# A recorder with its own list schedule takes the place of the framework's scheduler, on one core

## The chip, the cores and the metric

The kernel runs on one core of a Trainium2 chip. The core has TensorE (matmuls, in the profile PE, with its weight loads as PEld), VectorE (DVE), ScalarE (ACT), GpSimd (POOL) and SyncE (SP), which issues all DMA transfers here. Each engine takes its own instructions in a fixed order and waits on semaphores where an instruction needs another engine's or a transfer's result. The metric is the device time of one execution in microseconds; less is better.

## The reference

Two blocks over 2048 tokens of width 1024, all in float32. The first is an RMS norm, a pooling mixer and a residual; the second has modulation by a condition vector, a mixer of two halves and a residual.

```python
def pool_mixer(h, in_w, group_w, group_b, scale, out_w):
    u, gate = jnp.split(h @ in_w, 2, axis=-1)
    ug = u.reshape(b, s, POOL_GROUPS, POOL_GROUP_DIM)
    pooled = jnp.stack([trailing_mean(ug[:, :, g], w) ...], axis=2) - ug
    mixed = jnp.einsum('bsgc,gcd->bsgd', pooled, group_w) + group_b
    return (mixed.reshape(b, s, POOL_WIDTH) * scale * jax.nn.silu(gate)) @ out_w

def hybrid_mixer(h, w_in, b_in, conv_w, conv_b, rpb, ml_norm_w, w_out):
    proj = h @ w_in + b_in
    (na_q, na_k, na_v, na_z, ml_q, ml_k, ml_v, ml_o, ml_z, i_f, f_f, i_b, f_b) = jnp.split(proj, ...)
    na_out = neighbourhood_attention(na_q, na_k, na_v, rpb) * jax.nn.silu(na_z)
    qk = jax.nn.silu(centred_short_conv(jnp.concatenate([ml_q, ml_k], axis=-1), conv_w, conv_b))
    h_fwd = mlstm_chunkwise(mq, mk, mv, i_f, f_f)
    h_bwd = flip(mlstm_chunkwise(flip(mq), flip(mk), flip(mv), flip(i_b), flip(f_b)))
    hm = (h_fwd + h_bwd) * jax.nn.sigmoid(ml_o)      # then a layer norm per head, times silu(ml_z)
    return jnp.concatenate([na_out, ml_out], axis=-1) @ w_out
```

The attention has 8 heads of 64 on a grid of 32 rows by 64 columns; each token sees a window of 8 by 16, with a bias table. The mLSTM has 4 heads of 128, in both directions, chunk by chunk, with a state that each chunk hands to the next.

## The kernel before

Projections keep float32 accuracy with three matmuls each: weights and activations are split into a high and a low part (`split`, L140 on ScalarE and L141 on VectorE), and high x high, high x low and low x high are summed in PSUM. `load_w` (L153) brings a weight piece to `wraw` (2 buffers) by DMA and splits it into `whl` (4 buffers); `proj_cm` (L176 to L178), `proj_ko` (L165 to L167) and `tm_chunk` (L645 to L647, 256 columns) are the matmuls. Results go to the core's DRAM space and are read back by the stages that follow.

The program has these stages in time. Up to some 600 us the first block, in two halves of 1024 tokens. Then the second block's projections (`cm_chunk`, `tm_chunk`), the output half-stages (`out_half`, `out_block`) and the last norm. From some 830 us to 1890 us the projections are laced with two other kinds of work:

- 16 calls of `na_pair`, with 128 attention blocks between them. A block is: two matmuls of scores L735 into one PSUM bank; L738 on VectorE adds the bias tile `bt` and takes the row maximum; L741 on ScalarE is the exponential, L742 and L743 (POOL) the division; L749 on TensorE transposes; L752 (ScalarE), L753 (VectorE) and L754 (POOL) copy and split the result; L761 on TensorE multiplies with the values; L765 to L767 combine. Scores and transposes have one PSUM bank each, so the next block's L735 waits for L738, and its L749 for L752.
- 32 calls of `ml_step`. Each loads `ui` (L886, a row of 512 numbers for every partition, 256 KB), takes an exponential of it with `dec` as bias on ScalarE (L890), multiplies on POOL (L891, L892), takes another exponential (L894) and has small matmuls L916, L917, L924. `ml_gates` runs twice before such steps; it stores `d_u` and `d_dc` (L854 to L856), which `ui` and `dec` (L857) read back.

The order of each engine is set by the framework's scheduler. The program gives every operation a priority: a running number that `prio(base)` sets to another base for a block of code. The framework has its own model of the machine's times, takes the operations that are ready in it by priority, and writes each engine's instructions in that order. Attention and mLSTM bases (1900000 to 2550000) are mostly lower numbers, thus earlier, than those of the projections laced with them (2100000, 3000000, 3600000). In the output stage `out_norm` (L1026, the chain L186 to L191, and eight multiplications L1033 on POOL) is laced with `out_block` (L1056, the matmuls L1059 to L1061, L1063, and the sums L1069 on POOL).

Of the kernel before, what the change touches and what calls it, by code (L numbers as in the profile page):

```python
# [1 line left out]

# [4 lines left out]
F32 = mybir.dt.float32  # L7
F32R = mybir.dt.float32r
I32 = mybir.dt.int32
AF = mybir.ActivationFunctionType  # L10
ALU = mybir.AluOpType
PSUM = bass.MemoryType.PSUM
DRAM = bass.MemoryType.DRAM
# [48 lines left out]
KCW = (24, 32, 32, 24)  # L62
CC = (0, 1, 1, 2)
CCW = (24, 32, 24)


def body(nc, tc, a, out):
# [64 lines left out]

    d_b = [[dp.tile([8, 8, 16, (12, 16, 12)[e] * CCW[x]], F32, name=f"d_b{e}_{x}") for x in range(3)] for e in range(3)]
    mod = cp.tile([128, 24], F32, name="mod")
# [147 lines left out]
    def tables(x, tb, cs2):  # L282
        W = CCW[x]
        m0 = (0, 24, 56)[x]
        tv = tb[:, 0:23 * W].rearrange("p (a b) -> p a b", b=W)
        sh = (0, -8, -8)[x]

        def put(e, r, c0, a0, n):
            nc.sync.dma_start(d_b[e][x][:, r, :, c0 * W:(c0 + n) * W], tb[:, a0 * W:(a0 + n) * W])  # L289

        for h in range(8):
            nc.sync.dma_start(tv[h * 16:h * 16 + 16, 4:19],
                              bass.AP(tensor=a["rpb"].tensor, offset=16 + sh + 465 * h, ap=[[1, 16], [31, 15], [1, W]]))
        mk = cs2[:, C_CM + m0:C_CM + m0 + W]
        nc.gpsimd.tensor_tensor(out=tv[:, 4:19], in0=tv[:, 4:19],
                                in1=mk[:, None, :].to_broadcast([128, 15, W]), op=ALU.add)
        for r in range(4):
            put(0, 4 + r, 0, 8 + r, 8)
            put(2, r, 4, 4 + r, 8)
        for r0, r1 in ((0, 7), (15, 23)):  # L300
            nc.gpsimd.memset(tv[:, r0:r1], NEG)
        for r in range(8):
            put(1, r, 0, r, 16)
        for r in range(4):
            put(0, r, 0, 4 + r, 12)
            put(0, 4 + r, 8, 16, 4)
            put(2, 4 + r, 0, 4 + r, 12)
            put(2, r, 0, 0, 4)
# [963 lines left out]
```

## Time and profile before

| | before |
|---|---|
| median of 3 runs | 2161.88 us (2161.3 to 2164.38) |
| profiled execution | 2162.99 us, span 2161.2 us |
| TensorE busy | 1938.7 us (90%) |
| VectorE, ScalarE, POOL busy | 1266.6, 858.1, 676.7 us |
| DMA, all engines | 60.2% of the span, 406.18 MB |
| granted TensorE clock, mean | 0.946 |

The span is the time between the first and the last instruction. A matmul's busy time as the profile models it overlaps with the next one's, so the pace of TensorE is read from how many matmuls a stretch with no idle time holds. The granted clock has two levels, 1.2 and 2.4 GHz; 1.00 is the higher one, and a mean of 0.94 says how long each was granted. In lists of waits a row names who stood idle, what ended it, and the total, the count and the longest.

### The profile page before, as it was taken

To read this page: it belongs to the slowest core of one execution; us is meant where nothing else is said; L and a number is where in the kernel's file an instruction comes from. 1 tells how busy PE (TensorE), PEld (TensorE's weight loads), DVE (VectorE), ACT (ScalarE), POOL (GpSimd) and SP (SyncE) were. 2 spreads that over 40 slices of the span, in tenths; PEclk is the share of its full clock that TensorE was granted. 3 is DMA by queue.
4 is the path that set the end of the run, shared out by engine and by line. 5 is a ranking of instruction groups with operands and counts; after the bars stand their busy time and mean duration, and the time that the engine had idled before them with its cause. 6 is when DMAs were issued, how large, how long until landed. Compare 5 with 4: busy or idle time off the path is not lost.

```text
span 2161.2 us, 29857 instructions
## 1 busy us (share of the span) xinstructions
PE 1938.7 (90%) x10246; PEld 1659.6 (77%) x10246; DVE 1266.6 (59%) x2688; ACT 858.1 (40%) x1779; POOL 676.7 (31%) x624
## 2 busy tenths in 40 slices
PE   8999889999899799799999799878868788998997
PEld 6877768788789688789898687777867666877875
DVE  6654574786825474355556478544546668747565
ACT  3221233333422234444443344455444456544442
POOL 1110064353540002313233343344443345410252
PEclk8999999999999899999999899989989888999998
DMA  5354444333742239798777656788877688654553
GB/s 189 111 162 158 152 156 142 106 128 120 271 131 87 88 106 293 240 318 260 240 225 232 160 175 172 239 218 265 242 207 208 181 213 266 190 199 162 196 184 125
DMA packets 270920, 406.18 MB, mean 188 GB/s; under 512 B 28416, under 2 KB 158512, under 8 KB 270768
## 3 DMA queue, kind: packets, MB, share of 16 engines
q1 hardware_dynamic: 270768, 404.26, 60.2%
q8 instruction: 82, 1.34, 0.3%
q14 instruction: 70, 0.57, 0.1%
HBM read 292.35 MB, written 126.51 MB: 194 GB/s over the span
## 4 chain that ended last, share of the span: by engine, by line
PE 43%; DMA 29%; DVE 9%; issue 6%; SPq 5%; ACT 5%; POOL 3%; DVEq 0%; ACTq 0%; POOLq 0%
PE acc L178 9%; PE acc L177 9%; PE acc L176 9%; DMA ui<-d_u 6%; DMA bt<-d_b 4%; SPq L289 3%; DMA qt<-d_q 2%; DVE whl L141 2%; PE acc L645 2%; PE acc L646 2%; PE acc L647 1%; DMA wraw<-wtm 1%; DMA act<-d_z 1%; DMA d_h<-hs 1%; PE ps L761 1%
## 5 line engine op out<-in xcount | busy, mean ns | idle before, releaser
L176 PE MATMUL acc<-act,whl 128*128 128x512 f32 x1168 | 473.5, 405 | 28.2 <-ACT big L611 11.3
L178 PE MATMUL acc<-act,whl 128*128 128x512 f32 x1168 | 476.6, 408 | 2.3 <-DVE whl L141 2.3
L177 PE MATMUL acc<-act,whl 128*128 128x512 f32 x1168 | 476.3, 408 | 0.0
L141 DVE TENSOR_TENSOR whl<-wraw,whl 128x512 fp32r<-128x512 f32 (+1 forms) x272 | 245.8, 906 | 210.2 <-ACT whl L140 209.2
L140 ACT CAST whl<-wraw 128x512 fp32r<-128x512 f32 (+1 forms) x272 | 167.5, 618 | 365.0 <-PE acc L178 193.5
L176 PEld LDWEIGHTS acc<-act,whl 128*128 128x128 f32 x1168 | 231.2, 198 | 81.8 <-ACT whl L140 14.3
L178 PEld LDWEIGHTS acc<-act,whl 128*128 128x128 f32 x1168 | 227.5, 195 | 50.5 <-DVE whl L141 2.8
L177 PEld LDWEIGHTS acc<-act,whl 128*128 128x128 f32 x1168 | 227.9, 195 | 48.9 <-issue 0.4
L754 POOL TENSOR_TENSOR tt<-tr,tt 128x384 fp32r<-128x384 f32 (+3 forms) x128 | 158.9, 1242 | 242.8 <-DVE tt L753 186.9
L645 PE MATMUL acc<-whl,act 128*128 128x256 f32 (+1 forms) x736 | 212.4, 290 | 2.5 <-ACT whl L140 1.9
L646 PE MATMUL acc<-whl,act 128*128 128x256 f32 (+1 forms) x736 | 212.5, 290 | 0.0
L647 PE MATMUL acc<-whl,act 128*128 128x256 f32 (+1 forms) x736 | 212.3, 290 | 0.0
L645 PEld LDWEIGHTS acc<-whl,act 128*128 128x128 f32 x736 | 142.2, 194 | 3.9 <-ACT whl L140 2.3
L647 PEld LDWEIGHTS acc<-whl,act 128*128 128x128 f32 x736 | 142.8, 194 | 0.3
L646 PEld LDWEIGHTS acc<-whl,act 128*128 128x128 f32 x736 | 142.1, 193 | 0.8 <-issue 0.2
L176 PE MATMUL acc<-y,whl 128*128 128x512 f32 x304 | 120.7, 398 | 16.5 <-DVE h L462 14.5
L735 PE MATMUL ps<-kt,qt 128*128 128x384 f32 (+2 forms) x256 | 76.9, 377 | 55.4 <-DVE sm L738 48.0
L178 PE MATMUL acc<-y,whl 128*128 128x512 f32 x304 | 122.0, 401 | 0.0
L177 PE MATMUL acc<-y,whl 128*128 128x512 f32 x304 | 121.7, 400 | 0.0
L890 ACT ACTIVATE ui<-ui,dec 128x128 f32<-128x128 f32 x128 | 41.0, 390 | 186.5 <-DMA ui<-d_u 155.1
L743 POOL TENSOR_SCALAR bt<-bt,sm 128x384 f32<-128x384 f32 (+2 forms) x96 | 66.6, 693 | 148.8 <-DVE sm L742 131.6
L738 DVE CUSTOM_DVE_ANT_0 bt<-ps,bt 128x384 f32<-128x384 f32 (+2 forms) x96 | 52.0, 541 | 99.5 <-DMA bt<-d_b 86.1
(314 smaller groups left out, 3814.2 us busy)
## 6 DMA issues: line engine op xcount, KB each, us to landing
wraw<-wcm SPq DMA_DIRECT2D x96, 256.0 KB
qt<-d_q SPq DMA_DIRECT2D x64, 256.0 KB
big<-wada SPq DMA_DIRECT2D x24, 512.0 KB
vt<-d_nw SPq DMA_DIRECT2D x32, 384.0 KB
wraw<-wout SPq DMA_DIRECT2D x48, 256.0 KB
wraw<-wtm SPq DMA_DIRECT2D x40, 256.0 KB
bt<-d_b SPq DMA_DIRECT2D x48, 192.0 KB
wraw<-wgate SPq DMA_DIRECT2D x32, 256.0 KB
```

Of the source, the lines that this page charges most:

```text
L140: nc.scalar.copy(hi, src)
L141: nc.vector.tensor_tensor(out=lo, in0=src, in1=hi.bitcast(F32), op=ALU.subtract)
L176: nc.tensor.matmul(p, w(0, k), xs[k][:, 0, s], start=(k == 0), stop=False)
L177: nc.tensor.matmul(p, w(0, k), xs[k][:, 1, s], start=False, stop=False)
L178: nc.tensor.matmul(p, w(1, k), xs[k][:, 0, s], start=False, stop=(k == 7))
L289: nc.sync.dma_start(d_b[e][x][:, r, :, c0 * W:(c0 + n) * W], tb[:, a0 * W:(a0 + n) * W])
L645: nc.tensor.matmul(pu[u], hs[k][:, 0, s], w(0, kk), start=(k == 0 and (u == 0 or wd > 256)), stop=False)
L646: nc.tensor.matmul(pu[u], hs[k][:, 0, s], w(1, kk), start=False, stop=False)
L647: nc.tensor.matmul(pu[u], hs[k][:, 1, s], w(0, kk), start=False, stop=(k == 7 and (u == 1 or wd > 256)))
L735: nc.tensor.matmul(s[:, 0:n], qt[:, x, cb].rearrange("p a b -> p (a b)"), kv, start=(x == 0), stop=(x == 1))
L743: nc.gpsimd.tensor_scalar(out=pt[:, 0:n], in0=pt[:, 0:n], scalar1=sm[:, 3:4], scalar2=0.0, op0=ALU.mult, op1=ALU.add)
L754: nc.gpsimd.tensor_tensor(out=lo, in0=tr, in1=hi.bitcast(F32), op=ALU.subtract)
```

## The change

The body of the kernel is not edited. It is run on a recorder (`Order`) whose engines note each call, with its line, its priority, what it reads and writes, and a cost; `schedule` then plans all engines at once, and `emit` writes the instructions in the order of their planned start, under a mode of the framework in which each engine keeps the order that it is given. Priorities and buffers are those of before, and each tile is still given its buffer in the order of the program. The line numbers of the body are 399 higher after the change (L735 becomes L1134).

The plan is a list schedule: at each moment the free engine that can start earliest takes the operation with the lowest priority number among those that are ready. An operation is ready when its last producer has ended by the plan, plus 120 ns, plus a margin: 900 ns for readers on TensorE, 150 ns on VectorE, ScalarE and POOL, and a further 1200 ns behind a transfer. A transfer lands 2300 ns behind 1.5 times its own share of the DMA engines, which serve one transfer after another in the plan, with at most 8 in flight.

```diff
+PE, DVE, ACT, POOL, SP = range(5)
+SLACK = (900.0, 150.0, 150.0, 150.0, 0.0)
+LAT = 120.0
+DMA_LAT = 2300.0
+DMA_SLACK = 1200.0
+LANES = 8
...
+    def cost(self, r, outs, ins):
...
+            if ins[0].dtype == F32R:
+                return 6.0 + 0.437 * n
+            return max(224.0, 20 + 1.7 * n) if n > 1 else 224.0
...
+            r.dma = (runs * 30.0 + size * 4 / 30.0) / 16
+            return 330.0 + 0.35 * max(0, runs - 128)
+        if r.eng == ACT:
...
+            c = 195.0 + 0.84 * n
...
+            return 155.0 + 1.06 * n + (60.0 if not isinstance(r.kw.get("scalar", 1.0), float) else 0.0) + (
+                80.0 if "accum_out" in r.kw else 0.0)
+        if r.fn == "tensor_tensor":
+            return 80.0 + 2.4 * n
+        return 200.0 + 1.0 * n
...
+    def schedule(self):
...
+            best = None
+            for e in range(5):
+                t = max(free[e], now)
+                if not avail[e]:
+                    if not future[e]:
+                        continue
+                    t = max(t, future[e][0][0])
+                if best is None or t < best[0]:
+                    best = (t, e)
...
+            if e == SP and len(lanes) >= LANES and lanes[-LANES] > t:
+                r.ready = max(r.ready, lanes[-LANES])
+                push(r)
+                continue
...
+            r.start = t
+            free[e] = t + c
+            r.end = t + c
+            if r.dma is not None:
+                dma_free = max(dma_free, t) + r.dma
+                r.end = max(dma_free, t + r.dma * 1.5) + DMA_LAT
+                lanes.append(r.end)
...
+                if x.eng == e and r.dma is None:
+                    t1 = r.end
+                else:
+                    t1 = r.end + LAT + SLACK[x.eng] + (DMA_SLACK if r.dma is not None else 0.0)
...
+    def emit(self):
...
+        with self.tc.manual_schedule():
+            for r in sorted(self.order, key=lambda r: (r.start, r.idx)):
...
@@ -1266,6 +1665,10 @@
     with _tile.TileContext(nc, schedule_with_timeline_sim=True) as tc:
-        body(nc, tc, a, out)
+        with ExitStack() as ctx:
+            o = Order(nc, tc, ctx)
+            body(o.nc, o, a, out)
+            o.schedule()
+            o.emit()
```

The order changes on every engine. Three places follow. The first is the end of the second `ml_gates` (in the trace of before at 1219 us). ScalarE before, from L848, the last operation of the gates there:

```order
L848 ACTIVATE mlg<-mlg 64x128 x2
L741 ACTIVATE bt,sm<-bt,sm 128x384
L752 COPY tr<-ps 128x384
L890 ACTIVATE ui<-ui,dec 128x128 x4
L765 COPY ot<-ps 64x8x16
L741 ACTIVATE bt,sm<-bt,sm 128x288
```

ScalarE there now (L1247 is L848, L1289 is L890):

```order
L1247 ACTIVATE mlg<-mlg 64x128 x2
L1164 COPY ot<-ps 64x8x16
L1140 ACTIVATE bt,sm<-bt,sm 128x288
L1151 COPY tr<-ps 96x384
L1164 COPY ot<-ps 64x8x16
L1140 ACTIVATE pt,sm<-pt,sm 128x512
L1151 COPY tr<-ps 96x384
L1164 COPY ot<-ps 64x8x16
L1140 ACTIVATE bt,sm<-bt,sm 128x512
L1151 COPY tr<-ps 96x384
L1164 COPY ot<-ps 64x8x16
L539 CAST whl<-wraw 128x512
```

The reader of `ui`, L1289, follows as the next row; it has moved behind ten operations of attention blocks and a weight cast, where two stood. SyncE at the same place before:

```order
L856 DMA d_dc<-mlg 128x1
L854 DMA d_u<-mlg 128x128
L855 DMA d_dc<-mlg 128x1
L720 DMA vt<-d_nw_127 128x3x256
L886 DMA ui<-d_u 128x4x128
L857 DMA dec<-d_dc 128x256
L726 DMA bt<-d_b_0_214 128x288
```

SyncE there now (L1125 is L726, L1285 is L886):

```order
L1125 DMA bt<-d_b_1_193 128x512
L1255 DMA d_dc<-mlg 128x1
L1119 DMA vt<-d_nw_107 96x3x256
L1102 DMA qt<-d_q_82 64x1024
L1253 DMA d_u<-mlg 128x128
L1254 DMA d_dc<-mlg 128x1
L1102 DMA qt<-d_q_82 64x1024
L1096 DMA kt<-d_k_86 128x1024
L1083 DMA d_mv<-big 128x2x256
L1285 DMA ui<-d_u 128x4x128
```

A `bt` load now stands ahead of the stores of the gates, and three transfers between those and the load of `ui`, where one stood. The second place is TensorE in the mixed stretch. Before, the two nearest pairs of scores L735 have 13 rows between them; these are the first of one such place:

```order
L735 MATMUL ps<-kt,qt 128x384 x2
L167 MATMUL acc<-act,whl 128x512
L761 MATMUL ps<-tt,vt 128x256 x2
L924 MATMUL ps<-wv,ks 128x129 x4
L761 MATMUL ps<-tt,vt 128x256 x2
L749 MATMUL ps<-ident,bt 128x128 x4
```

Eight projection matmuls follow there, and then the next L735. One of the near places now (L1134 is L735, L1160 is L761, L1044 to L1046 are projections):

```order
L1134 MATMUL ps<-kt,qt 128x384 x2
L1160 MATMUL ps<-tt,vt 128x256 x4
L1044 MATMUL acc<-whl,act 128x272
L1045 MATMUL acc<-whl,act 128x272
L1046 MATMUL acc<-whl,act 128x272
L1134 MATMUL ps<-kt,qt 128x288 x2
```

Here seven matmuls stand between two blocks' scores. The third place is POOL in the output stage, before:

```order
L1016 TENSOR_TENSOR big<-big 128x1024 x7
L1069 TENSOR_TENSOR big<-big,hr 128x512 x3
L1069 TENSOR_TENSOR big<-big,hb 128x512
L1033 TENSOR_TENSOR yr<-yr,big 128x1024 x8
L1069 TENSOR_TENSOR big<-big,hb 128x512 x6
```

POOL there now (L1432 is L1033, L1468 is L1069):

```order
L1415 TENSOR_TENSOR big<-big 128x1024 x7
L1468 TENSOR_TENSOR big<-big,hr 128x512 x2
L1432 TENSOR_TENSOR yr<-yr,big 128x1024 x2
L1468 TENSOR_TENSOR big<-big,hr 128x512
L1432 TENSOR_TENSOR yr<-yr,big 128x1024 x2
L1468 TENSOR_TENSOR big<-big,hb 128x512
```

The eight multiplications are no longer one run; two stand between one sum and the next.

## Rows read from the trace of the kernel before

**Rows 1.** The page, its first line and the busy time of TensorE (us, share of the span, instructions).

```profile
span 2161.2 us, 29857 instructions
PE 1938.7 (90%) x10246; PEld 1659.6 (77%) x10246; DVE 1266.6 (59%) x2688; ACT 858.1 (40%) x1779; POOL 676.7 (31%) x624
```

**Rows 2.** Busy time by stretch: from:to and length in us, then busy us and instructions of each engine, the granted clock, the DMA engines' mean busy share and GB/s. The first row is a stretch without idle time, the others are the four stages.

```profile
486.00:540.00 54.00, 54.00 (x236) 44.18 (x235) 36.02 (x34) 19.48 (x31) 20.75 (x8) 1.00 0.35 118
...
0.00:54.00 54.00, 43.76 (x177) 34.53 (x178) 35.52 (x45) 20.28 (x23) 8.71 (x9) 0.84 0.55 189
54.00:810.00 756.00, 711.52 (x3295) 590.38 (x3294) 455.70 (x545) 226.43 (x313) 205.60 (x121) 0.97 0.42 137
810.00:1890.00 1080.00, 941.60 (x5723) 838.74 (x5722) 616.21 (x1861) 503.53 (x1277) 392.34 (x454) 0.94 0.76 227
1890.00:2161.00 271.00, 241.87 (x1057) 195.94 (x1055) 159.22 (x238) 107.84 (x167) 70.05 (x41) 0.94 0.51 174
```

**Rows 3.** Waits of TensorE between 810 and 1890 us, the two longest: who, for whom, us in total, times, longest us.

```profile
PE ps L735 <- DVE sm L738: 48.0, 17, 12.2
PE ps L902 <- ACT ks L899: 11.5, 3, 5.5
```

**Rows 4.** Waits of ScalarE in the same stretch, the one for `ui` and one of the two for `dec`.

```profile
ACT ui L890 <- DMA ui<-d_u: 147.5, 27, 9.5
...
ACT ui L890 <- DMA dec<-d_dc: 13.8, 1, 13.8
```

**Rows 5.** Waits of VectorE in the same stretch.

```profile
DVE bt L738 <- DMA bt<-d_b: 86.1, 24, 14.2
...
DVE sm L742 <- ACT bt L741: 46.4, 39, 9.1
```

**Rows 6.** Pieces of the chain that ended last, loads of `ui` alone: start us, us from issue to landing, what.

```profile
853.49 11.38 DMA ui<-d_u
869.91 9.92 DMA ui<-d_u
...
1230.27 8.68 DMA ui<-d_u
...
1473.26 15.29 DMA ui<-d_u
...
1510.84 5.20 DMA ui<-d_u
...
1691.62 11.73 DMA ui<-d_u
```

**Rows 7.** Instructions in order of time behind the second `ml_gates`, by engine (SyncE, ScalarE, VectorE, TensorE): start us, us, engine, line, operation, idle time before and what ended it.

```profile
1219.21 0.34 SPq L855 DMA_DIRECT2D d_dc<-mlg  x1
...
1228.35 0.37 SPq L886 DMA_DIRECT2D ui<-d_u  x1
...
1229.37 0.37 SPq L726 DMA_DIRECT2D bt<-d_b  x1
...
1236.95 1.28 ACT L890 ACTIVATE ui<-ui,dec 128x128 f32<-128x128 f32 x4 [13.82 <-DMA dec<-d_dc]
...
1237.42 0.46 DVE L738 CUSTOM_DVE_ANT_0 bt<-ps,bt 128x288 f32<-128x288 f32 x1 [14.21 <-DMA bt<-d_b]
...
1237.94 0.85 PE L735 MATMUL ps<-kt,qt 128*128 128x288 f32 x2 [12.20 <-DVE sm L738]
1238.59 0.41 PE L647 MATMUL acc<-whl,act 128*128 128x256 f32 x1
1238.80 0.41 PE L645 MATMUL acc<-whl,act 128*128 128x256 f32 x1
```

**Rows 8.** The same view around 1705 us (ScalarE, VectorE, TensorE).

```profile
1703.37 1.28 ACT L890 ACTIVATE ui<-ui,dec 128x128 f32<-128x128 f32 x4 [6.12 <-DMA ui<-d_u]
...
1705.39 0.16 DVE L742 RECIPROCAL sm<-sm 128x1 f32<-128x1 f32 x1 [6.47 <-ACT pt L741]
...
1706.20 1.01 PE L735 MATMUL ps<-kt,qt 128*128 128x384 f32 x2 [6.62 <-DVE sm L738]
```

**Rows 9.** Groups of instructions: line, engine, operation, count, then busy us, mean ns of one, and idle us before them with what ended it.

```profile
L141 DVE TENSOR_TENSOR whl<-wraw,whl 128x512 fp32r<-128x512 f32 (+1 forms) x272 | 245.8, 906 | 210.2 <-ACT whl L140 209.2
L140 ACT CAST whl<-wraw 128x512 fp32r<-128x512 f32 (+1 forms) x272 | 167.5, 618 | 365.0 <-PE acc L178 193.5
...
L754 POOL TENSOR_TENSOR tt<-tr,tt 128x384 fp32r<-128x384 f32 (+3 forms) x128 | 158.9, 1242 | 242.8 <-DVE tt L753 186.9
...
L743 POOL TENSOR_SCALAR bt<-bt,sm 128x384 f32<-128x384 f32 (+2 forms) x96 | 66.6, 693 | 148.8 <-DVE sm L742 131.6
L738 DVE CUSTOM_DVE_ANT_0 bt<-ps,bt 128x384 f32<-128x384 f32 (+2 forms) x96 | 52.0, 541 | 99.5 <-DMA bt<-d_b 86.1
...
L752 ACT COPY tr<-ps 128x384 f32<-128x384 f32 (+3 forms) x128 | 68.1, 532 | 88.9 <-POOL tt L754 82.8 <-PE ps L749 4.8
```

**Rows 10.** POOL in order of time in the output stage, and pieces of the chain just after it.

```profile
2083.26 22.13 POOL L1033 TENSOR_TENSOR yr<-yr,big 128x1024 f32<-128x1024 f32 x8 [3.64 <-DMA big<-d_no]
2105.35 4.30 POOL L1069 TENSOR_TENSOR big<-big,hb 128x512 f32<-128x512 f32 x3
...
2109.70 1.41 PE L200 MATMUL ps<-ones,big 128*128 128x1 f32 x8 [2.97 <-POOL big L1069]
...
2111.75 0.43 PE acc L1060
2112.18 0.43 PE acc L1061
```

More of the change, by code (lines that the diff above doesn't have):

```diff
@@ L1 @@
+import sys
+import types
 from contextlib import ExitStack, contextmanager
@@ L64, with bits @@
 CCW = (24, 32, 24)
+PE, DVE, ACT, POOL, SP = range(5)
[4 more added lines that the diff above has]
+LANES = 8
+BIG = 1 << 62
+def bits(off, dims):
+    m = 1 << off if off >= 0 else 0
+    for st, n in dims:
+        if st == 0 or n == 1:
+            continue
+        if st < 0:
+            m >>= -st * (n - 1)
+            st = -st
+        k = 1
+        while k < n:
+            j = min(k, n - k)
+            m |= m << (j * st)
+            k += j
+    return m
@@ new lines, with __init__, __getattr__, call @@
+class Rec:
+    __slots__ = ("eng", "fn", "args", "kw", "line", "cost", "prio", "idx", "tiles", "npred", "succ", "ready", "end",
+                 "start", "dma", "table")
+class LTile:
+    __slots__ = ("tag", "left", "slot", "done", "seq", "acc", "pool", "make", "real")
+class Slot:
+    __slots__ = ("tile", "free")
+    def __init__(self):
+        self.tile, self.free = None, 0.0
+class Eng:
+    def __init__(self, o, num, real):
+        self.o, self.num, self.real = o, num, real
+    def __getattr__(self, name):
+        def call(*args, **kw):
+            self.o.record(self.num, name, args, kw, sys._getframe(1).f_lineno)
+        return call
@@ new lines, with __init__, __enter__, __exit__ @@
+class Recorder:
+    def __init__(self, o, nc):
+        self.tensor, self.vector = Eng(o, PE, nc.tensor), Eng(o, DVE, nc.vector)
+        self.scalar, self.gpsimd, self.sync = Eng(o, ACT, nc.scalar), Eng(o, POOL, nc.gpsimd), Eng(o, SP, nc.sync)
+class Pool:
+    def __init__(self, o, name, kw):
+        self.o, self.name, self.kw, self.real, self.recs, self.end = o, name, kw, None, 0, 0.0
+    def __enter__(self):
+        self.o.pools[self.name] = self
+        return self
+    def __exit__(self, *a):
+        return False
+    def tile(self, shape, dtype, **kw):
+        o = self.o
+        tag = f"{self.name}.{kw.get('tag', kw['name'])}"
+        if tag not in o.tags:
+            o.tags[tag] = [Slot() for _ in range(kw.get("bufs", self.kw["bufs"]))]
+            o.left[tag] = 0
+        k = f"t{len(o.tiles)}"
+        h = o.fake.dram_tensor(k, tuple(shape), F32, kind="Internal").ap()
+        lt = LTile()
+        lt.tag, lt.left, lt.slot, lt.done, lt.seq, lt.acc, lt.pool = tag, 0, None, 0.0, -1, [], self
+        lt.make, lt.real = (shape, dtype, kw), None
+        o.tiles[k] = lt
+        return h if dtype == F32 else h.bitcast(dtype)
```

245 lines of the change are left out of this document (added).

## The prediction

> **What bounds the kernel now.** I read the busy times first, then the same by stage, then who waits for whom in the worst stage, then two places in order of time. TensorE is busy for 1938.7 of 2161.2 us [rows 1]. Where nothing holds it back it issues 236 matmuls in 54.00 us at a granted clock of 1.00, one 512-column matmul each 54.00 / 236 = 0.229 us; that is the pace to compare with [rows 2]. By stage, the idle time of TensorE (stretch less busy) is 10.2 us in the head, 756.00 - 711.52 = 44.5 us in the first block, 1080.00 - 941.60 = 138.4 us in the stretch from 810 to 1890 us, and 271.00 - 241.87 = 29.1 us in the output stage [rows 2]. So the mixed stretch, where attention blocks and mLSTM steps are laced into projections, holds 62% of the idle time. Its granted clock is 0.94: 0.06 x 1080 = 65 us of full-speed clock are withheld there, some in idle time, the rest from matmuls just after it.
>
> Work to fill the gaps is not missing there, since projections are still queued behind each wait. What is missing is order. The longest wait of TensorE is for L738, VectorE's reading of the scores, 48.0 us in 17 places [rows 3]; VectorE waits for the bias tile `bt` (86.1 us) and for ScalarE's exponential (46.4 us) [rows 5]; and ScalarE waits 147.5 us in 27 places for `ui`, the 256 KB load of an mLSTM step [rows 4]. From issue to landing `ui` took 5.20 us once and 8.68 to 15.29 us in the other pieces of the chain shown [rows 6].
>
> Two places show how these are one thing. At 1691.62 us `ui` is issued and takes 11.73 us [rows 6]. ScalarE has L890, its reader, next in its row and stands 6.12 us; L741, an exponential of an attention block, is behind it; VectorE's L742 waits 6.47 us for that, L738 of the next block is behind L742, and TensorE stands 6.62 us before L735 [rows 8]. One late load stops three engines, since each takes its work in a fixed order. At 1219 us it is SyncE that is in order: the loads of `ui`, `dec` and `bt` stand behind a wait for a store and are issued from 1228.35 us on; ScalarE waits 13.82 us, VectorE 14.21 us, TensorE 12.20 us. The matmuls after it are 0.21 us apart where 256 columns take half of 0.229, so the clock is at its lower level, 1.2 GHz [rows 7].
>
> **The change, part by part.** No instruction is added or dropped; each engine has the same instructions in another order. So every term is a wait that goes, comes or moves.
>
> *The costs it plans with* are near this trace. Its formulas give 625 ns for a weight cast (618 measured), 518 ns for L752 (532), 642 ns for L738 (541); too short are L141 with 698 ns (906), L754 with 1002 (1242) and L743 with 584 (693) [rows 9]. The two last lie on one attention block's way back to TensorE and are 0.35 us short together; 0.90 us of margin stand before each TensorE reader. I cost these errors at nothing as long as that margin lasts.
>
> *Late loads, the main gain.* For `ui` the code reckons 4.56 us to landing in an empty queue and puts the reader 1.47 us behind that, 6.0 us after the issue at the earliest. Measured are 8.68 to 15.29 us but for one row [rows 6], so the plan clears part of most waits. In the place of the 1219 us stall the new order of SyncE has three other transfers between the stores and `ui` and a `bt` load ahead of them, and ScalarE has ten attention operations and a weight cast between L848 and L890 where it had two operations: the scores' readers then run while `ui` flies, and the 12.20 us should go. Elsewhere the reader moves less. Bounds: nothing gained, or all 138.4 us of idle time and 65 us of clock. I take half the idle time, 69 us, since the plan's 6.0 us covers about half of the middle of the rows (11 us), and 25 us of clock, less than half of the 65 because shorter stalls also lower it.
>
> [...]
>
> *The first block* (54 to 810 us) keeps nearly the order that it had. Of 44.5 us I take 8; bounds 0 and 20.
>
> *The output stage.* POOL does eight multiplications L1033 in one go, 22.13 us, and the sums L1069 stand behind them; TensorE waits 2.97 us for the last and runs at the lower clock after it, 0.43 us per matmul in place of 0.229 [rows 10]. Now L1033 alternates with L1069 in twos. That frees 2.97 us and some 15 x 0.2 = 3 us: 6 us, bounds 0 and 10. Against it, VectorE's chain L186 to L191 and six others now stand before the next weight split; the splits were a piece ahead, so I cost it at 3 us, 0 to 10.
>
> *The price: less cover on TensorE.* Counted over the 128 attention blocks in the two orders, the matmuls between a block's scores and the next block's were never fewer than 20, and 30 at the middle; now the middle is 21, and in 31 of 127 cases there are fewer than 12. Between a block's transposes and the next one's, 18 of 127 are under 12 where none was. Eleven matmuls of 256 columns are 11 x 0.115 = 1.3 us, while L738 alone takes 0.54 us and L752 0.53 us [rows 9], before either hands over. So 49 places have little cover. If all hold, the price is nothing; if each stalls as the 17 of before did, 48.0 / 17 = 2.8 us [rows 3], it is 49 x 2.8 = 137 us. The change cannot gain here. I take 35 us, 0.7 us a place: nearer to nothing, since these places were planned from costs that the rows bear out, and since the attention work ends earlier, with 1231 TensorE instructions after it in place of 803, all projections that ran without idle time before.
>
> *Sum:* -69 - 25 - 8 - 6 + 3 + 35 = -70 us. The profiled execution took 2162.99 us, 1.8 us of it outside its span, and 1.1 us over the median of 2161.88; that makes 2093 us on its scale and **2092 us** on the median's.
>
> **The rivals.** *First, slower: the cover is gone.* An order fixed from planned costs has no slack but its margins. When a `ui` lands 5 us late, ScalarE still stands, and now the next scores are 12 matmuls away in place of 30. Price: 137 us of stalls at the 49 places, and a quarter of that, 34 us, for the clock, against gains of 108 us: 2162 + 171 + 3 - 108 = 2228 us. It decides when the 49 places stall over 1.8 us on the mean (108 / 49 / 1.25). For it speaks that all `ui` rows but one are above the plan's 6.0 us; against it, that ScalarE waited 5.5 us on the mean (147.5 / 27) and is now given later readers.
>
> *Second, nothing to speak of: the loads stay as late.* DMA queues are busy for 0.76 of this stretch already [rows 2]; if attention work runs closer, its loads do too, and each lands later by what the reader was moved. A quarter of the main gain remains, 24 us, with 14 us elsewhere against 38 us of price: 2162 us.
>
> *Third, the margins suffice everywhere,* all of 138 and 65 us go and the price stays: 2162 - 203 - 14 + 38 = 1983 us. [...]
>
> *Fourth, that the order is not kept.* The built orders show that it is, on every engine; I give it no chance of its own.
>
> **How the numbers follow.** The forecast gets 0.56, its own range 2045 to 2140 (main gain from 45 to 130 us, price from 10 to 70). The first rival gets 0.28, the second 0.09, the third 0.07. A measurement of this kernel tells about 0.2% (4 us) from no change. Faster: 0.56 + 0.07 and 0.03 of the second, 0.66. Same: 0.05, from the second and the forecast's upper end. Slower: 0.29. The range goes up to 2205, which takes in two thirds of the first rival, and down to 2030: about 0.10 is left out above and 0.09 below.
>
> **What would show it.** Right: ScalarE's wait for `ui` near 75 us in place of 147.5; the 12 us stall after the second gate stage gone; TensorE idle near 100 us from 810 us to the end of attention and the granted clock there at 0.96; after the last attention block a stretch of 280 us at 0.229 us per matmul. Wrong by the first rival: TensorE's waits for L738, L752 and L767 in over 60 places and over 100 us together. Wrong by the second: `ui` rows above 14 us, with ScalarE's wait for it unchanged. Wrong in the price's size: many waits under 1 us with the clock at full speed, which would make it cheap, or waits for weight splits (L141), which I put at 3 us.

## The result, and the profile after

The changed kernel takes 2180.43 us, the median of 4 runs (2177.81 to 2184.62), against 2161.59 us for the kernel before on the same chip: a ratio of 1.0092, 95% interval 1.0066 to 1.0118. It is slower by 0.9%, where 3% faster was forecast. The profiled execution took 2179.49 us, its span is 2177.7 us.

The page, first line and TensorE's busy time, which answers to [rows 1]:

```profile
span 2177.7 us, 29691 instructions
PE 1949.4 (90%) x10246; PEld 1653.7 (76%) x10246; DVE 1300.9 (60%) x2688; ACT 867.2 (40%) x1779; POOL 683.0 (31%) x624
```

TensorE is idle for 2177.7 - 1949.4 = 228.3 us, 222.5 before. Its busy time rose by 10.7 us with the same 10246 instructions. Some 2 us of that are in the 64 transposes L976, which took 290 ns each and as L1375 now take 319 ns. Stalls so short that they lie under a matmul's modelled end would show like this; no row settles whether the rest is of that kind.

Busy time of the four stretches of [rows 2], and then of two parts:

```profile
0.00:54.00 54.00, 42.49 (x180) 34.22 (x181) 34.84 (x44) 20.21 (x23) 10.47 (x9) 0.84 0.52 184
54.00:810.00 756.00, 715.05 (x3330) 592.68 (x3329) 458.36 (x552) 229.40 (x321) 199.27 (x121) 0.98 0.43 141
810.00:1890.00 1080.00, 930.30 (x5614) 815.80 (x5613) 644.33 (x1890) 509.29 (x1285) 405.94 (x462) 0.93 0.77 228
1890.00:2161.00 271.00, 258.02 (x1109) 207.88 (x1107) 156.65 (x184) 106.34 (x149) 64.83 (x30) 0.98 0.46 155
...
1370.00:1860.00 490.00, 395.47 (x2361) 342.77 (x2360) 305.61 (x1008) 242.29 (x654) 201.14 (x236) 0.91 0.75 215
...
1944.00:2052.00 108.00, 108.00 (x468) 87.74 (x467) 69.22 (x68) 45.66 (x60) 16.20 (x6) 1.00 0.43 146
```

The mixed stretch, which was to lose half of its idle time, gained some: 1080.00 - 930.30 = 149.7 us, 138.4 before, and the granted clock went from 0.94 to 0.93. Once attention is over, 108 us pass without a gap, 108.00 / 468 = 0.231 us per matmul. So projections that could have filled gaps run by themselves at the end. TensorE's idle time is largest from 1370 to 1860 us, 94.5 us. The kernel before stood 91.7 us there, so the part that the change was to mend most is as it was:

```profile
1370.00:1860.00 490.00, 398.35 (x2378) 354.16 (x2377) 281.13 (x954) 243.35 (x655) 209.59 (x245) 0.90 0.80 228
```

Who waits there? TensorE's, ScalarE's and VectorE's waits between 810 and 1890 us, which answer to [rows 3 to 5]:

```profile
PE ps L1148 <- ACT tr L1151: 21.6, 18, 3.3
PE ps L1134 <- DVE sm L1137: 21.0, 18, 3.8
PE ps L1323 <- issue: 18.8, 7, 5.4
PE acc L1044 <- ACT whl L539: 11.1, 3, 5.7
PE ps L1134 <- DMA qt<-d_q: 9.6, 2, 7.7
...
ACT ui L1289 <- DMA ui<-d_u: 72.7, 25, 5.3
...
DVE bt L1137 <- DMA bt<-d_b: 21.9, 10, 4.6
```

What the change was costed for did happen: ScalarE's wait for `ui` fell from 147.5 to 72.7 us, VectorE's for `bt` from 86.1 to 21.9 (the row shown; with the one for the tile `pt` from 114.7 to 39.9), and TensorE's longest wait, for L738 (now L1137), from 48.0 to 21.0 us. But other waits took its place, many of them 1 to 3 us long: for the copy of the transposes (L752, now L1151), for links of the mLSTM chain (L924, now L1323; the profile does not show what ended the 18.8 us of its row), and a kind that the kernel before hardly had, a projection waiting for its own weight (L140, now L539). Over the whole span TensorE's waits for `whl` come to 51.4 us in 21 places, 13.9 us in 5 before. The longest row of before, and the two longest after beside the one for L1044 above:

```profile
PE acc L176 <- ACT whl L140: 9.7, 2, 7.0
...
PE acc L575 <- ACT whl L539: 13.1, 4, 5.3
PE acc L1460 <- DVE whl L540: 11.7, 6, 4.6
```

The longest of them in the worst part, in order of time, from the issue of the weight's load on:

```profile
1470.23 3.11 SPq L552 DMA_DIRECT2D wraw<-wtm  x1
...
1485.54 0.62 ACT L539 CAST whl<-wraw 128x512 fp32r<-128x512 f32 x1 [2.84 <-DMA wraw<-wtm]
1486.19 0.69 DVE L540 TENSOR_TENSOR whl<-wraw,whl 128x512 fp32r<-128x512 f32 x1 [2.85 <-ACT whl L539]
1486.21 0.79 PE L1044 MATMUL acc<-whl,act 128*128 128x256 f32 x2 [5.75 <-ACT whl L539]
...
1487.31 0.41 PE L1046 MATMUL acc<-whl,act 128*128 128x256 f32 x1
1487.53 0.41 PE L1044 MATMUL acc<-whl,act 128*128 128x256 f32 x1
```

The weight's load lands, ScalarE casts it at once, and TensorE, idle for 5.75 us, starts as soon as the cast is done; the matmuls after it are 0.22 us apart, the lower clock. The projection that should have covered an attention block's wait was itself not ready. Here it was the load that came late, 15.3 us behind its issue; that a split stands behind attention work, as most of what follows argues, is read from the plan and from edits, not from this place.

At the second `ml_gates`, the place of [rows 7], the stall is smaller and has changed its load:

```profile
1219.70 0.48 SPq L1102 DMA_DIRECT2D qt<-d_q  x1
1220.24 6.07 SPq L1096 DMA_DIRECT2D kt<-d_k  x1
1226.40 0.38 SPq L1083 DMA_DIRECT2D d_mv<-big  x1
1231.61 0.37 SPq L1285 DMA_DIRECT2D ui<-d_u  x1
...
1233.49 1.19 PE L1134 MATMUL ps<-kt,qt 128*128 128x512 f32 x2 [7.70 <-DMA qt<-d_q]
...
SPq L1285 <- DMA d_u<-mlg: 4.7, 1, 4.7
```

SyncE spends 6.07 us on the issue of one load. `ui` goes out only at 1231.61 us, behind a wait of 4.7 us for the store of `d_u` (the last row, from SyncE's waits between 1215 and 1240 us). TensorE stands 7.70 us in place of 12.20, now for `qt`, whose load was issued at 1219.70 us, ahead of the long issue.

### The profile page after: what moved, and what is told of

Read it like the earlier page. It is cut to its first block, busy times and chain, and to the rows that moved or that the text cites. A ratio compares the mean times of both kernels' runs of the same rounds, so it can differ in the third digit from the quotient of the medians.

```text
span 2177.7 us, 29691 instructions
## 1 busy us (share of the span) xinstructions
PE 1949.4 (90%) x10246; PEld 1653.7 (76%) x10246; DVE 1300.9 (60%) x2688; ACT 867.2 (40%) x1779; POOL 683.0 (31%) x624
## 5 line engine op out<-in xcount | busy, mean ns | idle before, releaser
L575 PE MATMUL acc<-act,whl 128*128 128x512 f32 x1168 | 468.8, 402 | 33.1 <-ACT whl L539 13.1
L577 PE MATMUL acc<-act,whl 128*128 128x512 f32 x1168 | 471.2, 405 | 3.0 <-DVE whl L540 2.3
L576 PE MATMUL acc<-act,whl 128*128 128x512 f32 x1168 | 471.5, 404 | 0.0
L540 DVE TENSOR_TENSOR whl<-wraw,whl 128x512 fp32r<-128x512 f32 (+1 forms) x272 | 246.2, 914 | 176.2 <-ACT whl L539 175.8
L539 ACT CAST whl<-wraw 128x512 fp32r<-128x512 f32 (+1 forms) x272 | 166.8, 620 | 377.4 <-PE acc L577 203.8
L575 PEld LDWEIGHTS acc<-act,whl 128*128 128x128 f32 x1168 | 228.5, 196 | 87.1 <-ACT whl L539 18.3
L577 PEld LDWEIGHTS acc<-act,whl 128*128 128x128 f32 x1168 | 224.2, 192 | 48.7 <-DVE whl L540 2.5
L576 PEld LDWEIGHTS acc<-act,whl 128*128 128x128 f32 x1168 | 224.4, 192 | 47.2
L1044 PE MATMUL acc<-whl,act 128*128 128x256 f32 (+1 forms) x736 | 211.7, 291 | 11.5 <-ACT whl L539 11.1
L1046 PE MATMUL acc<-whl,act 128*128 128x256 f32 (+1 forms) x736 | 211.1, 288 | 0.0
L1044 PEld LDWEIGHTS acc<-whl,act 128*128 128x128 f32 x736 | 141.3, 193 | 13.9 <-ACT whl L539 12.2
L1046 PEld LDWEIGHTS acc<-whl,act 128*128 128x128 f32 x736 | 142.2, 193 | 0.5
L1134 PE MATMUL ps<-kt,qt 128*128 128x384 f32 (+2 forms) x256 | 80.2, 389 | 33.5 <-DVE sm L1137 21.0
L1160 PE MATMUL ps<-tt,vt 128*128 128x256 f32 (+1 forms) x448 | 83.3, 304 | 16.5 <-DVE ot L1166 6.4
L1151 ACT COPY tr<-ps 128x384 f32<-128x384 f32 (+3 forms) x128 | 67.9, 530 | 61.2 <-POOL tt L1153 42.4
L1160 PEld LDWEIGHTS ps<-tt,vt 128*128 128x128 f32 (+1 forms) x448 | 69.8, 203 | 26.1 <-issue 8.6
```

The source lines that it names most:

```text
L539: nc.scalar.copy(hi, src)
L540: nc.vector.tensor_tensor(out=lo, in0=src, in1=hi.bitcast(F32), op=ALU.subtract)
L575: nc.tensor.matmul(p, w(0, k), xs[k][:, 0, s], start=(k == 0), stop=False)
L576: nc.tensor.matmul(p, w(0, k), xs[k][:, 1, s], start=False, stop=False)
L577: nc.tensor.matmul(p, w(1, k), xs[k][:, 0, s], start=False, stop=(k == 7))
L1044: nc.tensor.matmul(pu[u], hs[k][:, 0, s], w(0, kk), start=(k == 0 and (u == 0 or wd > 256)), stop=False)
```

## The experiments

The seventh is the kernel before with an edit, all others are the changed kernel with one. Each ratio is against the kernel before on the same chip, with its 95% interval. Five theories stand in what was expected:

- **A, weights:** the filler's weights come late, since `load_w` has the low priority of the projection that it serves.
- **B, thin cover:** less filler stands between links of attention, and planned costs plus 0.9 us don't cover real ones (the first rival of the prediction).
- **C, loads:** the readers of `ui` and `bt` still come too early (the second rival).
- **D, short costs:** the plan's costs of VectorE and POOL are too low.
- **E, chance:** any small edit gives another order, and this one was a bad draw.

### Four single causes

Weights first:

```diff
+            with prio(tc.cur_priority - 5000000):
                 raw = wp.tile([128, 544], F32, name="wraw", tag="wraw", bufs=2)[:, 0:kp * width]
                 nc.sync.dma_start(raw, src[:, k0 * width:(k0 + kp) * width])
                 w = wp.tile([128, 2, 544], F32R, name="whl", tag="whl", bufs=4)
                 split(w[:, 0, 0:kp * width], w[:, 1, 0:kp * width], raw, scale)
```

> The loads and splits of projection weights (the piece of code that brings a weight to wraw and splits it into whl) get priority numbers 5000000 lower, so that the plan takes them ahead of all else; everything else is the changed kernel. Theory A, weights: in the changed kernel TensorE stands 51.4 us in 21 places for a split weight, before it 13.9 us in 5; the filler that should cover attention is itself late because its weights have the filler's low priority. Then those waits fall back to under 15 us, the gaps of other kinds keep their size, and the time falls by some 37 us to about 2143 us, below the kernel before. Theory B, thin cover: the waits for weights only take the place of waits for attention links that would stand there anyway; the time stays within 10 us of 2180. Theory C, loads of ui and bt: no change either, 2175 to 2185, or a little worse, since weights go ahead of ui on the queue.

Measured 2104.32 us, ratio 0.9753 (0.9728 to 0.9779). That is A's direction, and the gain of 76 us is twice what it expected: the waits for weights fell from 51.4 to 16.6 us, those of attention matmuls (L735, L749, L761) and of the mLSTM's from 117.2 to 75.8 us as well.

```diff
-SLACK = (900.0, 150.0, 150.0, 150.0, 0.0)
+SLACK = (2500.0, 150.0, 150.0, 150.0, 0.0)
```

> The margin ahead of each reader on TensorE is 2500 ns in place of 900, nothing else. Theory B, thin cover: the waits of TensorE for links of attention blocks and mLSTM steps (74.6 us in 54 places and 42.6 us in 29 places) are mostly under 3 us each, so 1.6 us more margin takes away some 60 of these 117 us; the small stalls that hide in busy time (13 us more in the mixed stretch than before) go as well, and the time falls to about 2120 us. Theory A, weights: the filler still waits for its own weights, 51 us stay, attention waits fall a little: 2160 to 2175 us. Theory C, loads: 2170 to 2185 us, as ACT still stands for ui.

2142.72 us, ratio 0.9917 (0.9890 to 0.9944), a gain of 38 us, but not where B looks for it: waits for attention and mLSTM links stayed (82.7 and 41.9 us), those for weights fell to 10.8 us. A weight's reader is on TensorE too, so the margin reaches the filler's weights.

```diff
-DMA_SLACK = 1200.0
+DMA_SLACK = 4000.0
```

> The margin behind a transfer is 4000 ns in place of 1200, so a reader of ui is planned 8.8 us behind the issue in place of 6.0; nothing else. Theory C, loads still late: ScalarE's wait for ui (68.4 us in 24 places between 835 and 2046 us) falls below 20 us, VectorE's for bt (39.9 us in 18 places) below 15 us, and with them TensorE's waits by 30 us or more: about 2145 us. Theory A and theory B: readers of loads come later, each buffer is held 2.8 us longer, and with only two raw weight buffers the weights come later as well; TensorE's waits for weights grow over 51 us and the time is 2200 us or more.

2184.08 us, ratio 1.0111 (1.0088 to 1.0134). C falls: the wait for `ui` is 68.8 us between 835 and 2046 us, as it was (68.4), and that for `bt` 34.0 us in its two rows (39.9). The growth that A and B expected did not come either; the waits for weights are 43.1 us.

> Both: weights first, and 2500 ns ahead of readers on TensorE. If theory A and theory B each name a cost of its own, the gains of the two single edits add up (2143 and 2120 alone would make 2085 together). If one cost only shows in place of the other, the two together are no better than the better one by more than 10 us.

2115.36 us, ratio 0.9801 (0.9775 to 0.9828). The two gains do not add up: with weights first, the margin has nothing left to give. So B adds no cost to that of A; that the margin covers nothing of its own is not shown.

### Which half, and whose order

Splits only (the cast and the subtraction), or the load only:

```diff
+            with prio(tc.cur_priority - 5000000):
                 split(w[:, 0, 0:kp * width], w[:, 1, 0:kp * width], raw, scale)
```

> Only the splits of a weight (the cast on ScalarE and the subtraction on VectorE) get priority numbers 5000000 lower; its load keeps the number of the changed kernel. Theory A1, the turn on ScalarE and VectorE: the weights are in the buffer in time, and stand there behind attention work on the two engines. Then this alone gives nearly all that weights first gave (2104.32 us): 2100 to 2120 us. Theory A2, the turn on the queue: loads go out too late behind bt, ui and qt, and the splits have nothing to split: 2165 to 2185 us, as the changed kernel.

> The other half: only the load of a weight gets the lower number. Theory A1: the two raw buffers fill early and wait for their splits; TensorE's waits for weights stay near 51 us and the time near 2165 to 2185 us. Theory A2: 2100 to 2120 us.

Splits: 2105.73 us, ratio 0.9753 (0.9735 to 0.9770). Loads: 2141.11 us, ratio 0.9923 (0.9896 to 0.9950). It is the turn on ScalarE and VectorE (A1); an early load alone gives half, more than A1 expected of it.

> The kernel before, under the framework's scheduler, with weights first as in the run that gave 2104.32 us. If weights first is a gain of its own, whoever makes the order, this gives about 2105 to 2120 us as well. If the late weights are a trait of the new plan (before, TensorE waits for weights only 13.9 us in 5 places), this gains 14 us at most, 2145 to 2162 us, or loses, and the list schedule with weights first is worth the difference.

2175.86 us, ratio 1.0077 (1.0061 to 1.0093). Under the framework's scheduler the same priorities cost 0.8%; TensorE's waits for weights, small there anyway, go from 13.9 to 0.3 us and others grow. Late weights are a trait of the new plan.

```diff
-            return 155.0 + 1.06 * n + (60.0 if not isinstance(r.kw.get("scalar", 1.0), float) else 0.0) + (
+            return 155.0 + (1.5 if r.fn == "tensor_tensor" else 1.06) * n + (60.0 if not isinstance(r.kw.get("scalar", 1.0), float) else 0.0) + (
...
-            return 80.0 + 2.4 * n
-        return 200.0 + 1.0 * n
+            return 80.0 + 2.65 * n
+        return 200.0 + 1.5 * n
```

> Weights first, and three cost formulas nearer to the trace of the changed kernel: a two-tensor operation on VectorE with 1.5 ns an element in place of 1.06 (the weight subtraction takes 914 ns, the plan reckons 698), on POOL 2.65 in place of 2.4, and POOL's other operations 1.5 in place of 1.0 (L1142 takes 794 ns, the plan reckons 592). Theory D, short costs: what is left of waits for attention links and weights comes from links that the plan ends too early; true costs take 10 to 20 us off 2104.32. Theory A alone: within 6 us of 2104.32 us, since the margins already cover errors of 0.2 us.

2143.52 us, ratio 0.9920 (0.9902 to 0.9938): a miss for D and for the 6 us. Truer costs lost 39 of the 76 us. The longest of TensorE's waits is then one of the first block:

```profile
PE acc L575 <- DVE sg L821: 22.9, 9, 6.6
```

That was 10.3 us in 6 places with weights first alone. But the first block is the small part: against weights first alone TensorE idles 7 us more between 54 and 810 us and 23 us more between 810 and 1860 us. The plan has the loss too, as shown below under the plan itself; why truer costs make a longer plan was not settled.

### How much is chance

Two plans from the changed kernel and one from splits first, with `LAT` at 130 or 110 in place of 120 ns, and one without the margin behind a transfer (`DMA_SLACK = 0.0`):

> A control for how far the time of such a plan hangs on chance: the changed kernel with 130 ns between engines in place of 120, a change that means nothing for any wait but gives another plan. Theory A, late weights: TensorE's waits for weights stay between 35 and 65 us and the time stays within 12 us of 2180. Theory E, chance: any small change gives another order, the late weights of the changed kernel are its bad draw, and this comes out 20 us or more away from 2180, with waits for weights that do not follow the time.

> The same control to the other side: 110 ns in place of 120. Theory A: within 12 us of 2180. Theory E: 20 us or more away from it, and from the run with 130.

> The same control on the version with the splits of weights first (2105.73 us): 130 ns in place of 120. Theory A: within 12 us of 2106 and clear of both controls of the changed kernel. Theory E: it lies among them.

> The changed kernel without the margin behind a transfer (0 in place of 1200 ns), so a reader of ui is planned 4.8 us behind the issue in place of 6.0. If the margin is what took half of ScalarE's wait for ui away, that wait (68.4 us in 24 places between 835 and 2046 us) rises to 90 us or more, and the time by 10 us or more, to 2190. If the wait fell because attention work was put between a gate or an mLSTM step and the reader, whatever the margin, it stays at 60 to 80 us, as it did at 4000 ns (68.8 us), and the time stays within 12 us of 2180 or falls, since buffers come free sooner.

2165.47 us, ratio 1.0025 (1.0009 to 1.0041); 2167.17 us, 1.0032 (1.0017 to 1.0048); 2131.38 us, 0.9860 (0.9835 to 0.9886); 2178.20 us, 1.0078 (1.0056 to 1.0101). Ten nanoseconds that mean nothing move the time by 13 to 26 us, more than A expected. So most of the 0.9% is a draw; that the change brings no gain is not, since no plan with late weights came out below the kernel before unless its margins or its loads helped the weights. With weights or splits first all came out below, the worst at 2131 us with the plan's own costs.

The run with 110 ns and the one without the margin have only 18 and 18.8 us of waits for weights, and are hardly faster. So waits that name a weight are not the measure of the loss. The wait for `ui` was 61.5 us without the margin: with 0, 1200 and 4000 ns it is 61.5, 68.4 and 68.8 us. The margin is not what halved it.

### The plan itself

So I read the plan. It holds a start and an end for each operation, and TensorE's idle time in it, with whether the next projection's weight was split by then, can be read before any run. In the plan of the changed kernel TensorE idles 191.7 us, 155.7 us of that in gaps that open before the weight of the next projection in its order is split and the margin past. That count is a bound from above on what late weights cost in the plan: a gap that opens with the weight late can have other reasons too. A list schedule always takes ready work of the lowest number; what it puts between two links of attention is what is ready then. The splits, with the filler's high numbers, wait on two engines behind every ready attention operation. Four more edits test that.

The splits with 5000000 added in place of taken away; the splits first in the second block alone, by the condition below, or in the first block alone, by its opposite; and splits first with all readers of a projection's PSUM bank first as well:

```diff
+            with prio(tc.cur_priority - 5000000 * (src.tensor.name[:3] in ("wcm", "wtm", "wou"))):
                 split(w[:, 0, 0:kp * width], w[:, 1, 0:kp * width], raw, scale)
```

```diff
         r.npred, r.succ = len(preds), []
+        r.prio -= 5000000 * (eng != PE and any(t.tag == "pacc.acc" for t in r.tiles))
```

> The other dose: the splits of weights get numbers 5000000 higher, behind all else. In the mixed stretch they are last already (the plan there keeps its 113.4 us without a split weight), so the plan changes in the output stage only, where the norm's operations now all go ahead of the splits; its own idle time there grows by some 20 us. Theory A (late weights are what the plan lacks): 2190 to 2215 us, all of the loss after 1850 us, in waits of the output's first matmul for a split. Rival (the turn of the splits means little, the gain of splits first came with a lucky order): within 15 us of 2180 with no new waits there.

> Splits first for the weights of the second block alone (projections laced with attention, and the output). Theory A, through the plan: this is where the plan lacked filler, so it has nearly all of the gain: 2100 to 2135 us. Rival, the gain is spread or lies in the first block: over 2150 us.

> Splits first for the weights of the first block alone. Theory A: the mixed stretch keeps its lack of filler; 2160 to 2185 us, with the lower part of that from chance alone. Rival: under 2140 us.

> Splits first, and every operation of ScalarE, VectorE or POOL that reads a projection's PSUM bank gets a number 5000000 lower too. In the plan with the splits first, 45.9 us of TensorE's idle time pass with the filler's weight ready but no bank free. Theory A, carried on (whatever holds the filler back costs time): the plan idles 10 us less, and the time falls from 2105.73 to 2085 to 2100 us. If the weights were the only thing: 2100 to 2120 us; if the evictions push attention links back, over 2120 us.

Measured: 2199.30 us, ratio 1.0178 (1.0151 to 1.0204); 2109.75, 0.9762 (0.9736 to 0.9788); 2177.19, 1.0080 (1.0057 to 1.0104); 2104.51, 0.9734 (0.9707 to 0.9760). The stage is settled: the second block's weights give all but 4 us, the first block's 3 us, both less than a draw moves. The worst part, 1370 to 1860 us, with splits first in both blocks:

```profile
1370.00:1860.00 490.00, 425.78 (x2563) 370.59 (x2562) 320.79 (x1024) 264.07 (x683) 212.04 (x238) 0.94 0.82 235
```

in the second block alone:

```profile
1370.00:1860.00 490.00, 429.49 (x2576) 374.21 (x2575) 320.95 (x1026) 267.03 (x685) 212.27 (x238) 0.94 0.82 237
```

and in the first alone:

```profile
1370.00:1860.00 490.00, 396.79 (x2364) 342.61 (x2363) 306.44 (x1007) 241.89 (x654) 200.01 (x236) 0.90 0.76 216
```

In the first two, in the same 490 us, TensorE gets through some 200 more matmuls, stands 60.5 to 64.2 us in place of 94.5, and has the clock at 0.94 in place of 0.91. Splits last cost 19 us more than the changed kernel, with a new wait in the output stage. TensorE's two longest waits there:

```profile
PE acc L1458 <- ACT whl L539: 9.3, 12, 2.4
PE acc L1460 <- DVE whl L540: 7.2, 2, 6.5
```

The second of these is 11.7 us in 6 places in the changed kernel, and the first is new. That is some 5 us of idle time; the rest of the 19 us lies in clock and in other places, where A had put all of it here. The plan is 20.5 us longer. Evictions first gave nothing measurable over splits first, though the plan idles 10 us less.

The plans with the margins and costs of the change (a few ns of `LAT` aside), all in us:

| version | plan's span | TensorE idle in the plan | of it in gaps that open with the next weight late | measured |
|---|---|---|---|---|
| splits last | 2027.7 | 212.2 | 174.5 | 2199.30 |
| the changed kernel | 2007.2 | 191.7 | 155.7 | 2180.43 |
| first block's splits first | 2002.9 | 187.4 | 146.6 | 2177.19 |
| 110 ns | 1996.4 | 180.9 | 136.9 | 2167.17 |
| 130 ns | 1995.5 | 179.9 | 125.8 | 2165.47 |
| loads first | 1971.9 | 156.3 | 93.0 | 2141.11 |
| splits first, 130 ns | 1945.9 | 130.3 | 63.5 | 2131.38 |
| weights first | 1945.5 | 129.9 | 27.1 | 2104.32 |
| second block's splits first | 1945.2 | 129.7 | 76.0 | 2109.75 |
| splits first | 1940.9 | 125.4 | 66.8 | 2105.73 |
| splits and evictions first | 1931.2 | 115.7 | 60.7 | 2104.51 |

TensorE's busy time is the same in all plans, so the second and third columns move together. The measured time is the plan's span and 159 to 186 us more, all the way down. The fourth column is not the gain: weights first takes 129 us off it and 62 us off the idle time. Even the draws of 130 and 110 ns were in the plan: it is 11 to 12 us shorter, and the measured time 13 to 15 us. A spread of 27 us is left in the four rows near 1945 us, which the plan does not tell. The rule holds only among equal margins: without the margin behind a transfer the plan is 1977.3 us and the chip 201 us above it, with 4000 ns 2118.4 and 66 us, with 2500 ns ahead of TensorE 1996.0 and 147 us, with weights first as well 1975.1 and 140 us. The truer costs keep it: 1985.0 us, 159 us below the chip, and so their loss of 39 us against weights first is all in the plan.

The traces bear the plan out. Take each gap of TensorE, find the next projection matmul behind it, and look whether the split of the weight that it reads had ended when the gap opened. Between 810 and 1890 us it had not for 7.8 of 138.4 us of idle time in the kernel before, for 90.2 of 149.7 us in the changed kernel, and for 37.7 of 113.9 us with splits first. So the kernel before had its filler's weights ready and stood all the same, since its order had attention and mLSTM instructions next; in the new order the filler's weights were mostly not ready when a gap opened.

## Why the prediction was wrong

**The step that failed** is a sentence in front of the sum: that work to fill the gaps is not missing, since projections are still queued behind each wait. Queued is not ready. It was true of the kernel before, where the next weight was late for only 7.8 of 138.4 us of idle time, and the sum carried it over to the new order. There it was late for 90.2 of 149.7 us, so the plan had little to put there, and gaps and thin cover came out of the plan as it was written. Splits first, which changes no more than that, takes 75 us off and comes out at 2105.73 us, within 14 us of the forecast 2092. That nearness is no support for the sum: a draw moves the time by as much, and the terms did not come out one by one. No rival held the step; the last phrase of the prediction, waits for weight splits, put at 3 us, came nearest.

**Late loads, -69 - 25.** The cause was right: ScalarE's wait for `ui` was to be near 75 us and is 72.7. That TensorE's idle time would follow was not: the waits for L738 went down by 27 us and idle time between 810 and 1890 us went up by 11. The reason given, that 6.0 us of margin covers half of the loads, is refuted by the margins of 0 and 4000 ns; the place behind attention work, which the orders show, remains as the reason, argued only. The 12.20 us stall went to 7.70, not away.

**The first block, -8.** Right in size: between 54 and 810 us 35 more matmuls are done, 35 x 0.229 = 8.0 us. Of that only 3.5 us are idle time, of which the term spoke (44.5 to 41.0 us); the granted clock rose from 0.97 to 0.98.

**The output stage, -6 + 3.** The wait for L1069 is gone, and the weight split that was put at 3 us is 11.7 us in 6 places (L1460 waits for L540); even with splits first it is 10.2 us in 5, which was not followed up. By these two waits, 3.0 us gone and 11.7 come, the sign was wrong.

**Less cover, +35.** Not by the mechanism of the first rival: its signature, over 60 places and 100 us of waits for L738, L752 and L767, is 21.0 + 21.6 + 6.4 = 49.0 us in 39 places; before it was 48.0 + 10.5 + 5.9 = 64.4 us in 27. With splits first the three are 18.3, 8.5 and 0.7 us, so ready filler covers the last two; for L738 it does next to nothing.

**Costs at nothing, while the margin lasts.** Not confirmed: truer costs moved the time by 39 us, upwards, through another plan. The 0.35 us were misread as well, since the rows mix shapes: at 384 columns L754 takes 1.06 to 1.08 us and L743 0.76 us, 0.05 to 0.07 and 0.18 us more than the formulas.

**The second and third rivals** are out. The second (loads as late, 2162 us) wanted ScalarE's wait for `ui` unchanged, and it was halved. The third (the margins suffice, 1983 us) wanted it gone, and 72.7 us are left; the two loads of `ui` on the chain took 10.75 and 10.69 us, where the plan reckons 4.56.

## What to carry to other kernels

Filler covers a wait only if it is ready, so in a list schedule like this one what makes it ready (here the casts and subtractions of its weights) needs a priority above the work that it covers, not that of the filler. Under the framework's scheduler the same priorities, with the loads, cost 0.8%. A scheduler that plans all engines can be asked before any run where its own plan leaves the bound engine idle and what was missing there; from end to end of the table such idle time came back on the chip nearly one for one (96.5 us in the plan, 94.8 us measured), but only while the margins stayed the same. Try two or three plans that differ by nothing before reading a meaning into one per cent.

## What the runs showed of the hardware

A load's issue held SyncE for 6.07 us at 1220.24 us, the longest of the 1305 issues of the changed kernel, of which 861 took 0.3 to 0.5 us; in the kernel before the longest is a store with 6.14 us, at 1456.44 us. The traces do not show for what SyncE was held. The mean granted clock went with the idle time: 0.947 in the changed kernel, 0.959 with splits first and 0.944 with splits last.
